# Modulation sums with buffers of their own, one visit per step of the FFN, in five pieces

## The chip, the core and the metric

The kernel runs on one core of a Trainium2 chip. The metric is the device time of one execution in microseconds. The core has five engines that run their own instruction queues side by side: PE (matrix multiply, with PEld loading its stationary operand), DVE, ACT, POOL, and SP, which here issues most DMAs. An engine works through its queue in order, so an instruction that waits holds up everything queued behind it on that engine.

## The reference, cut to what matters

Two layers of a diffusion backbone on 256 latent tokens and 256 context tokens of width 1024. Each layer is: half-step SwiGLU FFN, token mixing (attention and S5), half-step SwiGLU FFN. Every normalisation is modulated: `norm(x) * (1 + scale) + shift`, and every residual is gated. Shift, scale and gate come from the conditioning vectors:

```python
mx = (silu(c)     @ w_mod[l] + b_mod[l]).reshape(B, 9, 1, D_MODEL)   # latent tokens
mc = (silu(c_ctx) @ w_mod[l] + b_mod[l]).reshape(9, D_MODEL)         # context tokens
hx = hx + 0.5 * mx[:, 2] * swiglu(modulate(hx, norm_g[l, 0], mx[:, 0], mx[:, 1]), ffn_w_gu[l, 0], ffn_w_down[l, 0])
```

`w_mod` is 1024 x 9216 per layer in float32, 38 MB. It is multiplied with only two vectors, so it can be done as a matrix product on PE, or as a sum of rows scaled by one number per partition on other engines. The FFN is 1024 to 2 x 2816 and back to 1024 for all 512 tokens.

## The kernel before, in words

Everything is written out by hand in program order; `plan` first lists all weight loads ("units") in the order of use. A unit is one `gu` tile (gate and up columns of one of the 22 blocks of 128 hidden columns, 1 MB), one `down` tile, one piece of `w_mod`, or another weight. `take` moves on to the next unit, asks SP for later ones (`load_to`), and returns the weights. The float32 weights in `raw` are split into a high and a low part (`spl`, two buffers): ACT rounds them (L265), DVE subtracts (L266), in two halves. PE then does three products per tile (`mm3`, L312 to L314). `ahead`, called by `take`, splits the next weight unit early if it is among the next two units.

The FFN (`ffn`) runs over 22 `gu` blocks in chunks of 8, 8 and 6. A block is 48 matmuls of 128x512; then ACT makes `sl` = silu (L756), DVE multiplies to `hv` (L758), ACT rounds it (L760) and POOL subtracts (L761) to give the split `hid`. After a chunk come four `down` units. After each block and each `down`, `fillers` visits the modulation units that stand next in the plan.

Eleven of the modulation vectors (`ELEM`) are not multiplied on PE. Their units are called `dvm`. A vector has four visits of two units; each unit has two tiles of 128x512 (`draw`, 512 KB, one DMA). Per tile DVE multiplies the rows by the latent vector's numbers and adds (L530 for the first, L532), ACT multiplies by the context vector's (L535, in place), POOL adds (L537). After four units half a vector is done: the partial sums `dacc` are summed over partitions by 8 small matmuls (L547, `total`) and transposed into place (L554, `finish`), 8 and 11 steps later. There are 24 such visits in the first FFN, 4 in the second, 16 in the third. In layer 1 the vectors 5 and 7 are needed for the latent tokens alone, so ACT and POOL have nothing to do there.

A "step" (`step`) comes after every third group of products in a block. It takes one entry of `dv` (what is left of the modulation), one of `q`, or one piece of the background work `bg`, which is `s5_prep`: the S5 matrices of the layer, many small operations on DVE and long ones on POOL (E at L1027 to L1032, CL at L1055 to L1057, BL at L1076 to L1078), and matmuls on them (L1064).

`load_to(i + 3)` counts all units, `dvm` ones too, and the `draw` tiles are in three buffers in the same SP queue as the raw weights.

Of the kernel before, what the change touches and what calls it, by code (L numbers as in the profile page):

```python
# [10 lines left out]
F32 = mybir.dt.float32  # L11
F32R = mybir.dt.float32r
AF = mybir.ActivationFunctionType
OP = mybir.AluOpType
# [6 lines left out]
T = 512  # L21
# [73 lines left out]
class Net:  # L95
    def __init__(self, nc, tc, I, out, es):
        self.nc, self.tc, self.I, self.out, self.es = nc, tc, I, out, es
        pool = lambda n, b=1, **kw: es.enter_context(tc.tile_pool(name=n, bufs=b, **kw))
        sb = lambda n, b=1: es.enter_context(lines(tc, name=n, bufs=b))
        self.const = sb("const")  # L100
        self.rawp = sb("raw", 3)
        self.splp = sb("spl", 2)
        es.enter_context(tc.tile_pool(name="top", bufs=1, side="right")).tile([128, 8], F32, name="top")
        self.pacc = pool("pacc", 4, space=PSUM)
        self.pt = pool("pt", 3, space=PSUM)
        self.pm = pool("pm", 1, space=PSUM)
        self.bank, self.turn = None, 0
        self.dram = pool("dram", 1, space=DRAM)
        c = self.const
        self.k = c.tile([128, K_END], F32, name="k")  # L110
        self.ident = self.k[:, K_ID:K_ID + 128]
        self.ones = self.k[:, K_ONE:K_ONE + 128]
        self.h = c.tile([128, KT, T], F32, name="h")
        self.xn = c.tile([128, 2, KT, T], F32R, name="xn")
        self.cs = c.tile([128, KT, 38], F32, name="cs")
        self.mh = c.tile([128, 8], F32, name="mh")
        self.sel = c.tile([128, 33], F32, name="sel")
        self.mod = [c.tile([128, 9, KT, 2], F32, name=f"mod{l}") for l in range(2)]
        self.A = [c.tile([128, 3, KT, 2], F32, name=f"A{l}") for l in range(2)]
        self.smT = [c.tile([128, 128], F32, name=f"smT{l}") for l in range(2)]  # L120
        self.kg = [c.tile([128, 4], F32, name=f"kg{l}") for l in range(2)]
        self.rho8 = [c.tile([128, 16], F32, name=f"rho8{l}") for l in range(2)]
        self.units = []
        self.dv = []
        self.fp = None
        self.bg = []
        self.q = []
        self.hold = False
        self.seaming = False
# [11 lines left out]
    def plan(self):  # L141
        I = self.I
        U = self.units

        def mod_units(l, m, us=range(4)):
            for u in us:
                if (l, m) in ELEM:
                    for v in (2 * u, 2 * u + 1):
                        n0, k0 = m * 1024 + v // 4 * 512, v % 4 * 2
                        src = I["w_mod"][l].rearrange("(k p) n -> p k n", p=128)[:, k0:k0 + 2, n0:n0 + 512]  # L150
                        U.append(("dvm", (l, m, v), [(slice(0, 1024), 2, src)], False))
                    continue
                src = I["w_mod"][l].rearrange("(k p) n -> p k n", p=128)[:, :, m * 1024 + u * 256:m * 1024 + u * 256 + 256]
                U.append(("mod", (l, m, u), [(slice(0, 2048), 8, src)], False))

# [12 lines left out]

        def ffn(l, f, fill, skip=0, between=None):
            fill = list(fill)  # L170
            for c in range(3):
                for j in range(max(skip, sum(CH[:c])), sum(CH[:c + 1])):
                    gu(l, f, j)
                    if j == 0 and between:
                        mod_units(*between)
                    if fill and j:
                        mod_units(*fill.pop(0))
                for u in range(4):
                    down(l, f, c, u)
                    if fill and (c, u) < (2, 2):  # L180
                        mod_units(*fill.pop(0))
            assert not fill
# [40 lines left out]
    def load_to(self, n):  # L223
        while self.loaded < min(n, len(self.units)):
            i = self.loaded
            kind, key, srcs, sp = self.units[i]
            if kind == "dvm" and self.fp is None:
                return
            if i < 10 and kind == "mod":
                raw = self.prop.tile([128, 2048], F32, name="pmod", tag="pmod", bufs=5)  # L230
            elif kind == "dvm":
                raw = self.fp.tile([128, 1024], F32, name="draw", tag="draw", bufs=3)
            else:
                raw = self.rawp.tile([128, 2048], F32, name="raw", tag="raw")
            for sl, k, src in srcs:
                if sl is None:
                    dst = raw.rearrange("p (k g n) -> p k g n", k=8, g=2)[:, :, k, :]
                elif sl == "glu":
                    dst = raw[16 * k:16 * k + 16, 0:1024].rearrange("p (b n) -> p b n", b=2)
                else:  # L240
                    dst = raw[:, sl].rearrange("p (k n) -> p k n", k=k)
                self.nc.sync.dma_start(dst, src)
            self.raws[i] = raw
            self.loaded += 1
# [24 lines left out]
    def take(self, kind, key, ahead=True):  # L269
        i = self.cur  # L270
        assert self.units[i][0] == kind and self.units[i][1] == key, (self.units[i][:2], kind, key)
        self.cur += 1
        if self.hold:
            self.load_to(min(i + 8, 11))
        else:
            self.load_to(i + 3)
        self.split(i)
        if ahead and not self.hold:
            self.ahead()
        self.raws.pop(i - 1, None)  # L280
        self.spl.pop(i - 1, None)
        return self.spl[i] if self.units[i][3] else self.raws[i]
# [43 lines left out]
    def step(self, n=1):  # L326

        for _ in range(n):
            if self.dv:
                g = self.dv.pop(0)  # L330
                if g:
                    g()
            f = self.q.pop(0) if self.q else None
            if f is not None:
                f()
            else:
                self.tick()
# [6 lines left out]

    def dv_flush(self):
        while self.dv:
            g = self.dv.pop(0)
            if g:
                g()

    def drain(self):
        while self.bg:
# [159 lines left out]
            us = [u] if alone else range(4)  # L512
            self.q.append(lambda: self.mod_finish(l, m, us, e))

    def dvm_unit(self, l, m, v):

        nc = self.nc
        half, r = v // 4, v % 4  # L520
        raw = self.take("dvm", (l, m, v)).rearrange("p (k n) -> p k n", k=2)
        ss = (1,) if l and m > 4 else (0, 1)
        if r == 0:
            self.dacc = {s: self.fp.tile([128, 512], F32, name=f"dacc{s}", tag=f"dacc{s}", bufs=2) for s in ss}
        acc = self.dacc
        for i in range(2):
            c0, c1 = (self.cs[:, 2 * r + i, 6 + s:7 + s] for s in range(2))
            first = r == i == 0
            if first:
                nc.vector.tensor_scalar(acc[1], raw[:, i], c1, None, op0=OP.mult)  # L530
            else:
                nc.vector.scalar_tensor_tensor(acc[1], raw[:, i], c1, acc[1], op0=OP.mult, op1=OP.add)  # L532
            if 0 in ss:
                x = acc[0] if first else raw[:, i]
                nc.scalar.activation(x, raw[:, i], AF.Copy, scale=c0)  # L535
                if not first:
                    nc.gpsimd.tensor_tensor(acc[0], acc[0], x, op=OP.add)  # L537
        if r < 3:
            return
        st = {}  # L540

        def total():
# [16 lines left out]
            nc.vector.tensor_tensor(dst.rearrange("p (j a) s -> p a j s", a=2), t, bc(b, [128, 2, 2, 2]), op=OP.add)  # L559
            self.mod_derived(l, m, k0, k0 + 4)  # L560

        self.dv_flush()
        self.dv += [None] * 7 + [total, None, None, finish]

    def mod_derived(self, l, m, k0, k1):
        nc = self.nc
# [166 lines left out]
    def ffn(self, l, f, halves, started, nxt=None):  # L733
# [3 lines left out]
        gate = 2 if f == 0 else 8  # L737
        hid = {}
        with lines(self.tc, name=f"ffn{l}{f}", bufs=1) as fp:
            self.fp = fp  # L740
            j0 = 0
            for ci, nf in enumerate(CH):
                for j in range(j0, j0 + nf):
# [10 lines left out]
                                    self.step()  # L754
                    sl = fp.tile([128, T], F32, name="sl", tag="sl", bufs=1)
                    nc.scalar.activation(sl[:, c], pg[:, c], AF.Silu)  # L756
                    hv = fp.tile([128, T], F32, name="hv", tag="hv", bufs=2)
                    nc.vector.tensor_tensor(hv[:, c], sl[:, c], pu[:, c], op=OP.mult)  # L758
                    hd = fp.tile([128, 2, T], F32R, name="hid", tag="hid", bufs=8)
                    nc.scalar.activation(hd[:, 0, c], hv[:, c], AF.Copy)  # L760
# [7 lines left out]
                    self.sq_begin()  # L768
                early = None
                if lastc:  # L770
                    self.dv_flush()
                for u in range(4):
                    w = early or self.take("down", (l, f, ci, u))
                    w = w[:, :, 0:nf * 256].rearrange("p s (k n) -> p s k n", k=nf)
# [22 lines left out]
                            self.step()  # L797
                    if ci == 0 and u == 0:
                        self.flush()
                    for i in range(2):  # L800
                        n = 2 * u + i
                        for s in halves:
# [31 lines left out]
    def s5_prep(self, l):  # L834
# [6 lines left out]
        with lines(self.tc, name=f"prep{l}", bufs=1, side="right") as pp:  # L841
# [4 lines left out]
            dma(par[0:16], I["s5_lam_re"][l].rearrange("d (a b) p -> (d a) (b p)", b=2))  # L846
            dma(par[32:48], I["s5_lam_im"][l].rearrange("d (a b) p -> (d a) (b p)", b=2))
            dma(ldt[64:80], I["s5_log_dt"][l].rearrange("d (a b) -> (d a) b", b=2))
            bl = [pp.tile([128, 16, 16], F32, name=f"bl{i}") for i in range(2)]
            for i, nm in enumerate(("s5_b_re", "s5_b_im")):  # L850
                nc.sync.dma_start(bl[i], I[nm][l].rearrange("d (a b) p m -> (b p) (d a) m", b=2))
            cr = pp.tile([128, 4, 2, 2, 64], F32, name="cr", tag="W")
# [824 lines left out]
```

## Time and profile before

| | us |
|---|---|
| median of 3 runs | 2185.57 (2183.81 to 2187.68) |
| the profiled execution | 2195.32 |
| its span, first to last instruction | 2193.5 |
| PE busy | 1984.7 (90%) |
| DVE busy | 1109.0 (51%) |
| ACT busy | 784.7 (36%) |
| POOL busy | 767.9 (35%) |

The mean granted clock of PE is 0.938 of full speed. Busy shares are averages over stages with different limits: the FFNs of the first layer run from about 50 to 545 us and from about 880 to 1270 us, those of the second from about 1290 to 1740 and from 2000 us on, and token mixing lies between.

### The profile page before, as it was taken

The page shows a single profiled execution, that of the slowest core. Times are in us where ns is not written, and L with a number is a line of the kernel's source. Part 1 is how long each engine was busy: PE and PEld are TensorE (multiplying, and loading weights), DVE is VectorE, ACT ScalarE, POOL GpSimd, SP SyncE. Part 2 cuts the span into 40 slices and gives each one's busy share as a digit, 9 for nine tenths or more (in the row PEclk, how much of TensorE's full clock was granted, in tenths as well). Part 3 has the DMA queues.
Part 4 walks back from the last instruction along what each step waited for, and adds up shares of the span by engine and source line. Part 5 has one row for each costly group of instructions (what it writes and reads, how often), then busy time and mean ns, then how long its engine had stood idle before and what let it go on. Part 6 is the DMA issues. An engine that isn't in the chain of part 4 may idle for free. (4 is left out here: it accounts for less than half of the span.)

```text
span 2193.5 us, 27710 instructions
## 1 busy us (share of the span) xinstructions
PE 1984.7 (90%) x10839; PEld 1600.1 (73%) x10839; DVE 1109.0 (51%) x1777; ACT 784.7 (36%) x1283; POOL 767.9 (35%) x789
## 2 busy tenths in 40 slices
PE   7788778889999999989999997778899999899999
PEld 5656556667889568768888875555678888668999
DVE  6566433543655774343332455555543465575554
ACT  4432333332435553331222343321222343455443
POOL 2348766431444404140100224864520244503000
PEclk9888888899999999989999998888899999899999
DMA  7533444454443103443333354344463344308663
GB/s 257 139 116 130 140 135 146 131 162 134 121 157 101 39 4 112 124 143 98 96 96 87 106 140 116 115 134 144 148 188 87 101 132 144 88 20 235 188 190 118
DMA packets 342278, 277.73 MB, mean 127 GB/s; under 512 B 30558, under 2 KB 311460, under 8 KB 342148
## 3 DMA queue, kind: packets, MB, share of 16 engines
q1 hardware_dynamic: 339184, 268.44, 41.2%
q0 software_dynamic: 1888, 7.31, 0.9%
q8 instruction: 85, 1.39, 0.3%
q14 instruction: 45, 0.37, 0.1%
q10 hardware_dynamic: 1076, 0.22, 0.1%
HBM read 263.39 MB, written 12.55 MB: 126 GB/s over the span
## 5 line engine op out<-in xcount | busy, mean ns | idle before, releaser
L312 PE MATMUL acc<-xn,spl 128*128 128x512 f32 (+1 forms) x1664 | 625.3, 376 | 96.3 <-ACT spl L265 87.9
L314 PE MATMUL acc<-xn,spl 128*128 128x512 f32 (+1 forms) x1664 | 617.2, 371 | 20.7 <-DVE spl L266 20.7
L313 PE MATMUL acc<-xn,spl 128*128 128x512 f32 (+1 forms) x1664 | 611.6, 368 | 1.9 <-DVE xn L429 0.2
L266 DVE TENSOR_TENSOR spl<-raw,spl 128x1024 fp32r<-128x1024 f32 (+2 forms) x312 | 391.9, 1292 | 231.5 <-ACT spl L265 229.6
L312 PEld LDWEIGHTS acc<-xn,spl 128*128 128x128 f32 x1664 | 329.0, 198 | 164.9 <-ACT spl L265 98.7
L265 ACT ACTIVATE spl<-raw 128x1024 fp32r<-128x1024 f32 (+3 forms) x344 | 323.8, 989 | 260.3 <-PE acc L314 138.5
L314 PEld LDWEIGHTS acc<-xn,spl 128*128 128x128 f32 x1664 | 327.4, 197 | 89.0 <-DVE spl L266 40.0
L761 POOL TENSOR_TENSOR hid<-hv,hid 128x512 fp32r<-128x512 f32 (+1 forms) x88 | 102.1, 1160 | 783.9 <-ACT hid L760 783.8
L313 PEld LDWEIGHTS acc<-xn,spl 128*128 128x128 f32 x1664 | 329.1, 198 | 54.6 <-DVE xn L658 4.3
L312 PE MATMUL acc<-hid,spl 128*128 128x512 f32 (+1 forms) x740 | 273.3, 369 | 28.8 <-ACT spl L265 28.8
L314 PE MATMUL acc<-hid,spl 128*128 128x512 f32 (+1 forms) x740 | 270.0, 365 | 10.5 <-DVE spl L266 10.5
L313 PE MATMUL acc<-hid,spl 128*128 128x512 f32 (+1 forms) x740 | 268.8, 363 | 0.0
L758 DVE TENSOR_TENSOR hv<-sl,acc 128x512 f32<-128x512 f32 (+1 forms) x88 | 54.6, 621 | 391.5 <-PE acc L314 344.6
L537 POOL TENSOR_TENSOR dacc<-dacc,draw 128x512 f32<-128x512 f32 x126 | 187.2, 1485 | 158.7 <-ACT draw L535 106.8
L822 DVE SCALAR_TENSOR_TENSOR h<-acc,mod,h 128x256 f32<-128x256 f32 x192 | 84.8, 478 | 226.4 <-PE acc L314 226.4
L760 ACT ACTIVATE hid<-hv 128x512 fp32r<-128x512 f32 (+1 forms) x88 | 50.8, 577 | 391.1 <-DVE hv L758 391.1
L312 PEld LDWEIGHTS acc<-hid,spl 128*128 128x128 f32 x740 | 144.0, 195 | 55.4 <-ACT spl L265 32.5
L314 PEld LDWEIGHTS acc<-hid,spl 128*128 128x128 f32 x740 | 144.3, 195 | 37.4 <-DVE spl L266 16.5
L532 DVE SCALAR_TENSOR_TENSOR dacc<-draw,cs,dacc 128x512 f32<-128x512 f32 x154 | 164.0, 1065 | 4.7
L313 PEld LDWEIGHTS acc<-hid,spl 128*128 128x128 f32 x740 | 144.5, 195 | 20.0
L266 POOL TENSOR_TENSOR spl<-raw,spl 128x768 fp32r<-128x768 f32 (+3 forms) x32 | 65.5, 2047 | 213.7 <-ACT spl L265 204.0
L535 ACT ACTIVATE draw<-draw,cs 128x512 f32<-128x512 f32 x126 | 91.0, 724 | 131.4 <-DVE dacc L532 83.2
(390 smaller groups left out, 2355.5 us busy)
## 6 DMA issues: line engine op xcount, KB each, us to landing
raw<-in_ffn_w_gu SPq DMA_DIRECT2D x176, 512.0 KB
draw<-in_w_mod SPq DMA_DIRECT2D x88, 512.0 KB
raw<-in_ffn_w_down SPq DMA_DIRECT2D x32, 1024.0 KB
raw<-in_w_mod SPq DMA_DIRECT2D x20, 1024.0 KB
raw<-in_ffn_w_down SPq DMA_DIRECT2D x16, 768.0 KB
raw<-in_w_in SPq DMA_DIRECT2D x16, 768.0 KB
pmod<-in_w_mod SPq DMA_DIRECT2D x8, 1024.0 KB
raw<-in_w_out SPq DMA_DIRECT2D x8, 1024.0 KB
```

Of the source, the lines that this page charges most:

```text
L265: nc.scalar.activation(s[:, 0, a:b], raw[:, a:b], AF.Copy)
L266: (nc.gpsimd if mix and b == n else nc.vector).tensor_tensor(s[:, 1, a:b], raw[:, a:b], s[:, 0, a:b].bitcast(F32), op=OP.subtract)
L312: mm(out, sl[0], sr[0], start=start, stop=False)
L313: mm(out, sl[0], sr[1], start=False, stop=False)
L314: mm(out, sl[1], sr[0], start=False, stop=stop)
L532: nc.vector.scalar_tensor_tensor(acc[1], raw[:, i], c1, acc[1], op0=OP.mult, op1=OP.add)
L535: nc.scalar.activation(x, raw[:, i], AF.Copy, scale=c0)
L537: nc.gpsimd.tensor_tensor(acc[0], acc[0], x, op=OP.add)
L758: nc.vector.tensor_tensor(hv[:, c], sl[:, c], pu[:, c], op=OP.mult)
L760: nc.scalar.activation(hd[:, 0, c], hv[:, c], AF.Copy)
L761: nc.gpsimd.tensor_tensor(hd[:, 1, c], hv[:, c], hd[:, 0, c].bitcast(F32), op=OP.subtract)
L822: self.nc.vector.scalar_tensor_tensor(self.h[:, n, c], ps[:, c], self.mod[l][:, gate, n, s:s + 1], self.h[:, n, c], op0=OP.mult, op1=OP.add)
```

## The change

A `dvm` unit is now one per visit, with four tiles; it no longer has loads in the list of units, and `load_to` is given a bound that counts three units other than `dvm`. The tiles of a visit are loaded by `dvm_load`, called at the start of the FFN and then at each visit for the next one, into four buffers of their own. The products and sums of a visit go into `dv` as five pieces, one per step; what is left is done at the next visit. The sum over partitions and the finish move to a list `late`, due 9 and 12 steps after the visit. To make room, `hv` has one buffer instead of two, and in `s5_prep` the two `bl` tiles share the buffers of tag "big".

```diff
@@ plan / mod_units
-                    for v in (2 * u, 2 * u + 1):
-                        n0, k0 = m * 1024 + v // 4 * 512, v % 4 * 2
-                        src = I["w_mod"][l].rearrange("(k p) n -> p k n", p=128)[:, k0:k0 + 2, n0:n0 + 512]
-                        U.append(("dvm", (l, m, v), [(slice(0, 1024), 2, src)], False))
+                    U.append(("dvm", (l, m, u), [], False))
+                    self.visits.setdefault(where[0], []).append((l, m, u))
@@ load_to / take
-            if kind == "dvm" and self.fp is None:
-                return
+            if kind == "dvm":
+                self.raws[i] = None
+                self.loaded += 1
+                continue
-                raw = self.fp.tile([128, 1024], F32, name="draw", tag="draw", bufs=3)
-            self.load_to(i + 3)
+            n, left = i, 3
+            while left and n < len(self.units):
+                left -= self.units[n][0] != "dvm"
+                n += 1
+            self.load_to(n)
@@ step
             if self.dv:
-                g = self.dv.pop(0)
-                if g:
-                    g()
+                self.dv.pop(0)()
+            for g in self.late:
+                g[0] -= 1
+            while self.late and self.late[0][0] <= 0:
+                self.late.pop(0)[1]()
@@ dvm_load, dvm_unit
+    def dvm_load(self):
+        if not self.todo:
+            return
+        l, m, u = self.todo.pop(0)
+        half, k0 = u // 2, u % 2 * 4
+        self.draws = []
+        for i in range(2):
+            raw = self.fp.tile([128, 2, 512], F32, name="draw", tag="draw", bufs=4)
+            n0 = m * 1024 + half * 512
+            self.nc.sync.dma_start(raw, self.I["w_mod"][l].rearrange("(k p) n -> p k n", p=128)[:, k0 + 2 * i:k0 + 2 * i + 2, n0:n0 + 512])
+            self.draws += [raw[:, 0], raw[:, 1]]
...
-        raw = self.take("dvm", (l, m, v)).rearrange("p (k n) -> p k n", k=2)
+        self.take("dvm", (l, m, u), False)
+        raws = self.draws
+        self.dv_flush()
+        self.dvm_load()
+        while r == 0 and len(self.late) > 2:
+            self.late.pop(0)[1]()
...
+        def parts(i):
+            if i < 4:
+                part1(i)
+            if i and 0 in ss:
+                part0(i - 1)
+
+        self.dv += [(lambda i=i: parts(i)) for i in range(4)]
+        if r == 0:
+            self.dv.append(lambda: parts(4))
             return
+        self.dv.append(lambda: parts(4))
...
-        self.dv_flush()
-        self.dv += [None] * 7 + [total, None, None, finish]
+        self.late.append([9, total, m])
+        self.late.append([12, finish, m])
@@ ffn
-            self.fp = fp
+            self.fp, self.todo = fp, self.visits.get((l, f), [])
+            self.dvm_load()
-                    hv = fp.tile([128, T], F32, name="hv", tag="hv", bufs=2)
+                    hv = fp.tile([128, T], F32, name="hv", tag="hv", bufs=1)
                 if lastc:
-                    self.dv_flush()
+                    self.late_flush()
                     if ci == 0 and u == 0:
                         self.flush()
+                        while any(g[2] == 2 for g in self.late):
+                            self.late.pop(0)[1]()
@@ s5_prep
-            bl = [pp.tile([128, 16, 16], F32, name=f"bl{i}") for i in range(2)]
+            bl = pp.tile([128, 2, 16, 16], F32, name="bl", tag="big", bufs=2)
+            bl = [bl[:, i] for i in range(2)]
```

## Rows read from the trace of the kernel before

**Rows 1.** The page: busy time by engine; one of the costliest groups (busy, mean ns).

```profile
PE 1984.7 (90%) x10839; PEld 1600.1 (73%) x10839; DVE 1109.0 (51%) x1777; ACT 784.7 (36%) x1283; POOL 767.9 (35%) x789
...
L537 POOL TENSOR_TENSOR dacc<-dacc,draw 128x512 f32<-128x512 f32 x126 | 187.2, 1485 | 158.7 <-ACT draw L535 106.8
```

**Rows 2.** Waits of PE, the longest: us in total, times, longest us.

```profile
PE acc L312 <- ACT spl L265: 116.7, 40, 5.5
PE acc L314 <- DVE spl L266: 31.2, 41, 1.6
PE t L1064 <- POOL CL L1057: 8.8, 2, 5.0
```

**Rows 3.** Timeline of one visit: start us, us, engine, line, operation, count, [idle before].

```profile
933.36 0.69 DVE L758 TENSOR_TENSOR hv<-sl,acc 128x512 f32<-128x512 f32 x1 [8.34 <-PE acc L314]
...
934.62 1.99 ACT L265 ACTIVATE spl<-raw 128x1024 fp32r<-128x1024 f32 x2
934.79 1.27 POOL L761 TENSOR_TENSOR hid<-hv,hid 128x512 fp32r<-128x512 f32 x1 [7.25 <-ACT hid L760]
...
935.71 0.79 PE L312 MATMUL acc<-xn,spl 128*128 128x512 f32 x1 [2.48 <-ACT spl L265]
...
937.19 0.79 PE L314 MATMUL acc<-xn,spl 128*128 128x512 f32 x1 [0.26 <-DVE spl L266]
...
938.20 4.00 DVE L532 SCALAR_TENSOR_TENSOR dacc<-draw,cs,dacc 128x512 f32<-128x512 f32 x4
938.21 0.63 PE L313 MATMUL acc<-xn,spl 128*128 128x512 f32 x1
...
938.64 0.63 PE L314 MATMUL acc<-xn,spl 128*128 128x512 f32 x1
```

**Rows 4.** Stretches: us, busy (instructions) of five engines, PE's granted clock, DMA, GB/s.

```profile
932.80:949.90 17.10, 14.35 (x49) 10.75 (x48) 7.08 (x7) 6.01 (x8) 7.31 (x5) 0.80 0.33 95
1020.00:1250.00 230.00, 230.00 (x1009) 189.20 (x1008) 76.57 (x88) 58.78 (x75) 22.07 (x17) 1.00 0.32 93
```

**Rows 5.** Three lines of the program, whole run: duration ns min/median/max.

```profile
L266 DVE TENSOR_TENSOR spl<-raw,spl x312: 681/1220/2443, 27.4 to 2181.3; 128x1024 fp32r<-128x1024 f32 x126, 128x768 fp32r<-128x768 f32 x24, 128x576 fp32r<-128x576 f32 x2, 128x864 fp32r<-128x864 f32 x2
L532 DVE SCALAR_TENSOR_TENSOR dacc<-draw,cs,dacc x154: 736/752/3533, 75.4 to 1600.6; 128x512 f32<-128x512 f32 x154
L537 POOL TENSOR_TENSOR dacc<-dacc,draw x126: 1262/1300/2167, 77.0 to 1457.5; 128x512 f32<-128x512 f32 x126
```

**Rows 6.** Waits of SP's DMA queue, the second longest.

```profile
SPq L242 <- POOL dacc L537: 545.6, 61, 28.5
```

**Rows 7.** The five stretches with visits, columns as in rows 4 (PE, PEld, DVE, ACT, POOL).

```profile
55.00:150.00 95.00, 76.16 (x284) 57.57 (x283) 53.62 (x113) 36.90 (x52) 34.59 (x30) 0.84 0.45 125
150.00:390.00 240.00, 191.37 (x803) 142.59 (x802) 115.54 (x159) 80.33 (x111) 169.19 (x182) 0.87 0.44 136
390.00:485.00 95.00, 76.57 (x309) 57.13 (x309) 45.31 (x62) 32.06 (x44) 36.43 (x28) 0.89 0.53 159
910.00:980.00 70.00, 58.74 (x210) 43.94 (x209) 28.30 (x30) 26.19 (x36) 24.63 (x18) 0.83 0.43 128
1310.00:1600.00 290.00, 230.36 (x941) 171.62 (x939) 166.23 (x241) 76.67 (x105) 168.49 (x176) 0.86 0.44 135
```

**Rows 8.** Timeline of one sum over partitions.

```profile
154.33 0.64 PE L547 MATMUL t<-dacc,sel 128*32 128x256 f32 x8
```

**Rows 9.** The same five stretches, line L313 alone: PE and PEld.

```profile
55.00:150.00 95.00, 38.11 (x88) 19.32 (x88) 0.84 0.45 125
150.00:390.00 240.00, 92.33 (x215) 46.15 (x215) 0.87 0.44 136
390.00:485.00 95.00, 38.00 (x91) 19.04 (x90) 0.89 0.53 159
910.00:980.00 70.00, 29.60 (x67) 14.98 (x66) 0.83 0.43 128
1310.00:1600.00 290.00, 111.78 (x258) 55.48 (x257) 0.86 0.44 135
```

More of the change, by code (lines that the diff above doesn't have):

```diff
@@ L123, in __init__ @@
         self.units = []
-        self.dv = []
+        self.dv, self.late = [], []
         self.fp = None
@@ L143, in plan @@
         U = self.units
+        self.visits, where = {}, [None]
         def mod_units(l, m, us=range(4)):
@@ L170, in ffn @@
             fill = list(fill)
+            where[0] = (l, f)
             for c in range(3):
@@ L226, in load_to @@
             kind, key, srcs, sp = self.units[i]
-            if kind == "dvm" and self.fp is None:
-                return
+            if kind == "dvm":
+                self.raws[i] = None
+                self.loaded += 1
+                continue
             if i < 10 and kind == "mod":
                 raw = self.prop.tile([128, 2048], F32, name="pmod", tag="pmod", bufs=5)
-            elif kind == "dvm":
-                raw = self.fp.tile([128, 1024], F32, name="draw", tag="draw", bufs=3)
             else:
@@ L346, in dv_flush, with late_flush @@
         while self.dv:
-            g = self.dv.pop(0)
-            if g:
-                g()
+            self.dv.pop(0)()
+    def late_flush(self):
+        self.dv_flush()
+        while self.late:
+            self.late.pop(0)[1]()
     def drain(self):
@@ L513, in mod_unit, with dvm_unit @@
             self.q.append(lambda: self.mod_finish(l, m, us, e))
-    def dvm_unit(self, l, m, v):
+    def dvm_load(self):
[9 more added lines that the diff above has]
+            self.draws += [raw[:, 0], raw[:, 1]]
+    def dvm_unit(self, l, m, u):
         nc = self.nc
-        half, r = v // 4, v % 4
-        raw = self.take("dvm", (l, m, v)).rearrange("p (k n) -> p k n", k=2)
+        half, r = u // 2, u % 2
+        self.take("dvm", (l, m, u), False)
+        raws = self.draws
         ss = (1,) if l and m > 4 else (0, 1)
+        self.dv_flush()
+        self.dvm_load()
+        while r == 0 and len(self.late) > 2:
+            self.late.pop(0)[1]()
         if r == 0:
@@ L525, in dvm_unit, with part1, part0 @@
         acc = self.dacc
[L526 to L530, printed above, removed]
-            else:
[L532 to L538, printed above, removed]
+        def part1(i):
+            c1 = self.cs[:, 4 * r + i, 7:8]
+            if r == i == 0:
+                nc.vector.tensor_scalar(acc[1], raws[i], c1, None, op0=OP.mult)
+            else:
+                nc.vector.scalar_tensor_tensor(acc[1], raws[i], c1, acc[1], op0=OP.mult, op1=OP.add)
+        def part0(i):
+            c0 = self.cs[:, 4 * r + i, 6:7]
+            x = raws[i] if r or i else acc[0]
+            nc.scalar.activation(x, raws[i], AF.Copy, scale=c0)
+            if r or i:
+                nc.gpsimd.tensor_tensor(acc[0], acc[0], x, op=OP.add)
+        def parts(i):
[6 more added lines that the diff above has]
+            self.dv.append(lambda: parts(4))
             return
+        self.dv.append(lambda: parts(4))
         st = {}
@@ L799, in ffn @@
                         self.flush()
+                        while any(g[2] == 2 for g in self.late):
+                            self.late.pop(0)[1]()
                     for i in range(2):
```

## The prediction

> **What bounds the kernel now.** I read the page first, then who waited for whom on PE, then the timeline of one stall, then tables by stretch. The page shows PE busy for 1984.7 of 2193.5 us [rows 1], so a change to the side work can only pay through PE's own stalls and its clock. PE's waits have one owner: 116.7 us until ACT has written the first half of a split weight (L265) and 31.2 us until DVE has written its remainder (L266), some 40 times each [rows 2]; nothing else is above 10 us. The timeline shows one such stall [rows 3]: when a unit's last matmul is done, DVE makes hv (933.36), then ACT splits the next weights (from 934.62), PE starts at 935.71, waits again for DVE's remainder until 937.19, and then takes 0.43 us per matmul (938.21 to 938.64). From 1020 to 1250 us, where no scaled sums run, PE takes 230 us for 1009 instructions, 0.228 each, at a granted clock of 1.00; the unit with the stall has 0.80 [rows 4]. So a stall costs its gap and then a spell at the lower of the two clock levels (1.2 instead of 2.4 GHz).
>
> A unit of 48 matmuls with a visit of the scaled sums behind it takes 17.10 us [rows 4]; without, 48 x 0.228 = 10.94. The difference, 6.16 us, is there once per visit, and the plan has 44 of them: 24 in the first FFN, 4 in the second, 16 in the third.
>
> Why it is there can be read in the code. `ahead` splits a unit only if it is among the next two. Before, a visit is two units (v = 2u, 2u+1), so the next weights are third in line and their split is left to the visit itself, behind hv and hid. In the clean stretch the next weights are at most second.
>
> **The change part by part.**
> One unit per visit, and a visit that doesn't split (`take(..., False)`): the next weights are now second in line, and their split is issued when the current unit is taken, a unit's time (11 us) before PE wants it. This is the edit that pays: up to 44 x 6.16 = 271 us if nothing else becomes late.
>
> Load window: three weight units ahead instead of three units of any kind, so the raw weights are asked for earlier. The split can't move without it. It costs no instruction.
>
> Scaled sums in five pieces: the same DVE, ACT and POOL instructions (four sums, four scalings, three or four adds per visit), handed out one piece per step. PE waits for none of them before the sum over partitions, so the order costs nothing while DVE and POOL have a unit's time for a visit's work: DVE 2 x 1.22 + 4 x 0.75 + 0.69 = 6.1 us, POOL 3.5 x 1.30 + 1.27 = 5.8 us, each alone [rows 3, 5]. What it costs where that cover is gone is the next part.
>
> Draws loaded at the visit before, two of 512 KB into four buffers: as many DMAs and bytes as now. On SP they stand in front of the next raw loads and wait for the last add and sum of the visit before. SP already waits 545.6 us for these adds [rows 6]. The ends: a gain (a draw no longer holds up a raw load within the visit), or a loss of POOL's backlog at each visit. I take zero, because the raw weights are asked for two units ahead; the loss is rival C. Traffic becomes 2.1 MB per 10.94 us, 192 GB/s, against at most 159 in a visited stretch now [rows 7]: a late DMA is kept in the upper end.
>
> The sum over partitions comes 9 steps after a visit and its finish 12 (before, 8 and 11): the same 8 small matmuls, 0.64 us [rows 8]. But the last piece is now issued only 4 steps before its sum, so PE would stand there for POOL: nothing if POOL is less than some 9 us behind, the rest of its backlog otherwise; I take nothing here and count POOL's load below. One hv buffer instead of two: DVE waits for POOL's remainder of the unit before, 1.27 us of work [rows 3] that starts a unit earlier; nothing unless POOL is a whole unit behind. b in the "big" buffers: read long before its buffer is wanted, nothing.
>
> **What is late next.** PE's floor in the five stretches with visits is three times the count of L313 [rows 9] at 0.228 us, and PE's other instructions of [rows 7] at 0.08 (0.64 for eight): 62, 160, 65, 47 and 190 us, 524 in place of 790. But POOL is busy 169.2 us in the second stretch and 168.5 in the fifth, DVE 115.5 and 166.2 [rows 7]: the preparation of S5 runs there too, paced by PE's steps, and is compressed with them. And DVE and POOL slow each other: four sums, 0.752 each at the median [rows 5], take 4.00 us with POOL's adds beside them [rows 3], and an add has a median of 1.300 and a mean of 1.485 [rows 1, 5].
>
> If DVE's splits and sums could not overlap with POOL at all, a visit would cost DVE 2 x 1.22 + 4 x 0.752 = 5.45 us on top of POOL's time. The second stretch holds 13 visits and 3.5 x 13 adds, which would be 0.185 shorter each: 169.2 - 8 + 71 = 232 us. The fifth holds 16; its preparation is lengthened too, and I take 150 us for POOL (an estimate, 11% off): 150 + 87 = 237. The other three, with little but visits, would be some us over their floor: 75, 70 and 50. What the rows show lies between full overlap and none, so I take the middle of floor and sum: 68, 196, 68, 49 and 214 = 595 us, 195 saved.
>
> The profiled execution took 2195.32 us, its span of 2193.5 and 1.8 around it; 2195.3 - 195 = 2000. It stood 0.45% above the median of the runs, 2185.57, so the median to expect is 2000 x 0.9956 = 1992 us.
>
> **The rivals.**
> A, PE's floor is reached everywhere. For it: PE waited for POOL (L1064) only 8.8 us in all [rows 2], and DVE and POOL have idle time in every stretch [rows 7]. Against: in the second, POOL's 169 us already exceed the floor of 160. 2195.3 - 266 = 1929, so 1921 us.
>
> B, DVE and POOL exclude each other, and the sums above hold: 75 + 232 + 70 + 50 + 237 = 664, 126 saved, 2069, so 2060 us. For it: the lengthened sums and adds. Against: in the fifth stretch the two are busy 334.7 us within 290 [rows 7], and it still moves on.
> [...]
>
> C, slower: SP becomes the bound. A draw load waits for POOL, the raw loads behind it wait too, and PE stands once POOL is further behind than the raw weights' lead, about a unit and a half or 16 us. It decides where POOL needs more than the present time per visit, 530/29 = 18.3 us in the second and fifth stretch. POOL has 169.2/13 = 13.0 us of work per visit; were all of it lengthened like its longest add against the mean (2.167 to 1.485), 18.9. Then 29 visits lose 0.6 us each, the other 15 gain nothing: 2213, so 2203 us. Against: POOL's 13.0 us hold much of that lengthening already.
>
> D, the split is issued early but runs late, since ACT stands before it for raw weights or in a piece: the stall stays, 2186 us. Against: in the clean stretch, with the same order, PE shows no gap [rows 4].
>
> **How the numbers follow.** Forecast 0.50 (its own range 1957 to 2026, half the way to A and to B), A 0.17, B 0.26, C 0.04, D 0.03. The likeliest gives 1992 us. The range takes in most of A and of B: 1930 to 2060. 0.2%, some 4 us, is what a measurement of this kernel tells from no change: faster 0.93, same 0.03, slower 0.04.
>
> **What would show it.** PE's waits for L265 and L266 fall from 148 us to under 40, and the granted clock of the visited stretches rises from 0.83 to 0.89 to above 0.95. L265 runs while PE is still in the unit before. L532's and L537's means rise. Where PE still waits, it is at L1064 or L547 for POOL, in the middle of the first and third FFN, and POOL is busy over 85% there. The forecast is wrong if the stretch from 910 to 980 us, which has no preparation, doesn't come down to about 49 us, or if L265 comes to wait for DMA at most visits.

## The result, and the profile after

The changed kernel takes 2035.68 us (median of 4 runs, 2031.85 to 2037.62) against 2186.62 of the kernel before in the same comparison (4 runs, 2183.81 to 2189.53). The ratio is 0.9307 (95% interval 0.9287 to 0.9328), so 151 us are saved. The time lies in the range, 44 us above the predicted 1992, beyond the forecast's own range (to 2026) and below rival B's 2060.

The page after: busy time by engine, and two of the costliest groups (busy, mean ns, then idle before them).

```profile
PE 1900.4 (94%) x10839; PEld 1556.5 (77%) x10839; DVE 1141.5 (56%) x1777; ACT 780.2 (38%) x1283; POOL 798.4 (39%) x789
...
L566 POOL TENSOR_TENSOR dacc<-dacc,draw 128x512 f32<-128x512 f32 x126 | 188.4, 1496 | 94.4 <-ACT draw L564 59.0
L559 DVE SCALAR_TENSOR_TENSOR dacc<-draw,cs,dacc 128x512 f32<-128x512 f32 x154 | 183.0, 1188 | 3.5
```

The instruction counts are those of [rows 1]; what changed is when the instructions run. L557, L559, L564 and L566 are the old L530, L532, L535 and L537; L316 to L318 the old L312 to L314; L586 the old L547; L1107 and L1100 the old L1064 and L1057.

PE's waits after (us in total, times, longest):

```profile
PE t L1107 <- POOL CL L1100: 57.2, 8, 17.8
PE b L586 <- POOL dacc L566: 6.1, 1, 6.1
...
PE acc L317 <- POOL hid L801: 4.2, 1, 4.2
PE t L593 <- ACT mev L588: 3.9, 2, 3.3
PE t L586 <- POOL dacc L566: 3.7, 1, 3.7
...
PE acc L318 <- DVE spl L266: 2.2, 5, 0.8
```

The two waits that owned the list in [rows 2], 148 us for L265 and L266, are gone: 2.2 us for DVE's remainder, and L265 is not in the list down to 1.5 us. In their place stands one that was 8.8 us before, PE's matmul of the S5 preparation waiting for POOL's CL, now 57.2.

One visit in the second FFN after (start us, us, engine, line, operation, count, [idle before]), to be laid beside [rows 3]:

```profile
845.46 1.99 ACT L265 ACTIVATE spl<-raw 128x1024 fp32r<-128x1024 f32 x2
846.54 2.61 DVE L266 TENSOR_TENSOR spl<-raw,spl 128x1024 fp32r<-128x1024 f32 x2 [1.65 <-ACT spl L265]
849.58 3.43 DVE L559 SCALAR_TENSOR_TENSOR dacc<-draw,cs,dacc 128x512 f32<-128x512 f32 x3
851.17 4.38 POOL L566 TENSOR_TENSOR dacc<-dacc,draw 128x512 f32<-128x512 f32 x3 [4.23 <-ACT draw L564]
852.50 3.44 SPq L534 DMA_DIRECT2D draw<-in_w_mod  x2
855.19 0.69 DVE L798 TENSOR_TENSOR hv<-sl,acc 128x512 f32<-128x512 f32 x1 [2.17 <-PE acc L318]
856.45 1.99 ACT L265 ACTIVATE spl<-raw 128x1024 fp32r<-128x1024 f32 x2
```

The split for the next unit runs at 845.46, 9.7 us ahead of this unit's hv (855.19). In [rows 3] it came 1.3 us behind hv, with PE already standing. Sums and adds lie under the matmuls.

The visited stretches after, bounded so that each holds the work of its counterpart in [rows 7]: each edge is the matmul of L317 that has the same number in PE's order as the matmul of L313 at the edge before. Columns as in [rows 4] (PE, PEld, DVE, ACT, POOL busy, granted clock, DMA, GB/s):

```profile
54.90:123.30 68.40, 64.36 (x282) 50.97 (x281) 42.87 (x95) 30.96 (x43) 24.48 (x21) 0.98 0.68 191
123.30:346.60 223.30, 176.54 (x804) 135.90 (x803) 150.20 (x178) 83.85 (x119) 194.06 (x188) 0.89 0.50 152
346.60:411.80 65.20, 65.20 (x307) 52.05 (x306) 48.09 (x59) 31.14 (x43) 43.66 (x30) 1.00 0.68 206
837.90:885.00 47.10, 47.10 (x213) 38.04 (x213) 25.88 (x28) 22.27 (x31) 20.37 (x15) 1.00 0.53 161
1213.90:1442.50 228.60, 197.49 (x938) 154.92 (x937) 166.81 (x242) 74.53 (x105) 172.17 (x173) 0.93 0.55 166
```

PE has the instruction counts of [rows 7] here, within three, so the prediction's floor holds as it stands: 62, 160, 65, 47 and 190 us. The third and fourth stretches are at their floor, at a granted clock of 1.00, and the first is 6 us over it. The second is 63 us over: PE stands 47 us (223.30 less 176.54) and works 17 us longer than the floor. The fifth is 39 over: 31 standing, 8 longer.

Where the second stretch stands, in the timeline (POOL's rows between two of PE's; same columns as above):

```profile
191.80 0.39 PE L318 MATMUL acc<-hid,spl 128*128 128x512 f32 x1
193.08 2.25 POOL L566 TENSOR_TENSOR dacc<-dacc,draw 128x512 f32<-128x512 f32 x1
195.29 1.59 POOL L1070 TENSOR_TENSOR te<-E,Pn 128x256 f32<-128x256 f32 x1
...
208.56 1.40 POOL L1100 TENSOR_TENSOR CL<-te,te 128x576 f32<-128x576 f32 x1 [0.96 <-DMA ed<-E]
210.01 0.64 PE L1107 MATMUL t<-CL,BB 128*32 128x128 f32 x2 [17.82 <-POOL CL L1100]
```

PE stands 17.8 us while POOL works through adds (L566) and the pieces of E (L1070 to L1075) before it comes to the CL that PE's next instruction wants. The stretches before and behind the pause (columns as above) show what it costs beside itself:

```profile
170.00:191.80 21.80, 21.14 (x100) 16.59 (x98) 17.20 (x26) 7.83 (x11) 20.63 (x33) 1.00 0.48 136
210.00:215.00 5.00, 0.69 (x6) 0.23 (x9) 0.00 (x0) 0.00 (x0) 4.82 (x4) 0.50 0.53 162
215.00:220.00 5.00, 5.00 (x24) 3.73 (x25) 0.88 (x2) 1.01 (x2) 4.63 (x5) 0.50 1.07 329
```

The granted clock is 1.00 (2.4 GHz) before the pause and 0.50 (1.2 GHz) in the two stretches behind it.

### The profile page after: what moved, and what is told of

Same layout as the page of the kernel before. It is cut to its first block, busy times and chain, and to the rows that moved or that the text cites. A ratio compares the mean times of both kernels' runs of the same rounds, so it can differ in the third digit from the quotient of the medians.

```text
span 2032.3 us, 27700 instructions
## 1 busy us (share of the span) xinstructions
PE 1900.4 (94%) x10839; PEld 1556.5 (77%) x10839; DVE 1141.5 (56%) x1777; ACT 780.2 (38%) x1283; POOL 798.4 (39%) x789
## 5 line engine op out<-in xcount | busy, mean ns | idle before, releaser
L316 PE MATMUL acc<-xn,spl 128*128 128x512 f32 (+1 forms) x1664 | 600.8, 361 | 8.6 <-ACT mv L1478 5.9
L317 PE MATMUL acc<-xn,spl 128*128 128x512 f32 (+1 forms) x1664 | 592.9, 356 | 1.9 <-DVE xn L438 0.2
L318 PE MATMUL acc<-xn,spl 128*128 128x512 f32 (+1 forms) x1664 | 592.0, 356 | 1.9 <-DVE spl L266 1.9
L266 DVE TENSOR_TENSOR spl<-raw,spl 128x1024 fp32r<-128x1024 f32 (+2 forms) x312 | 409.1, 1347 | 207.9 <-ACT spl L265 206.0
L265 ACT ACTIVATE spl<-raw 128x1024 fp32r<-128x1024 f32 (+3 forms) x344 | 323.7, 989 | 217.6 <-PE acc L318 184.9
L801 POOL TENSOR_TENSOR hid<-hv,hid 128x512 fp32r<-128x512 f32 (+1 forms) x88 | 107.8, 1225 | 662.8 <-ACT hid L800 662.7
L316 PEld LDWEIGHTS acc<-xn,spl 128*128 128x128 f32 x1664 | 315.7, 190 | 66.8 <-issue 10.8
L317 PEld LDWEIGHTS acc<-xn,spl 128*128 128x128 f32 x1664 | 315.7, 190 | 50.6 <-DVE xn L697 4.3
L318 PEld LDWEIGHTS acc<-xn,spl 128*128 128x128 f32 x1664 | 315.8, 190 | 50.0 <-DVE spl L266 4.1
L317 PE MATMUL acc<-hid,spl 128*128 128x512 f32 (+1 forms) x740 | 265.0, 358 | 4.2 <-POOL hid L801 4.2
L316 PE MATMUL acc<-hid,spl 128*128 128x512 f32 (+1 forms) x740 | 267.7, 362 | 0.0
L318 PE MATMUL acc<-hid,spl 128*128 128x512 f32 (+1 forms) x740 | 264.7, 358 | 0.3 <-DVE spl L266 0.3
L566 POOL TENSOR_TENSOR dacc<-dacc,draw 128x512 f32<-128x512 f32 x126 | 188.4, 1496 | 94.4 <-ACT draw L564 59.0
L559 DVE SCALAR_TENSOR_TENSOR dacc<-draw,cs,dacc 128x512 f32<-128x512 f32 x154 | 183.0, 1188 | 3.5
L564 ACT ACTIVATE draw<-draw,cs 128x512 f32<-128x512 f32 x126 | 91.0, 723 | 196.7 <-DVE dacc L559 152.3
L317 PEld LDWEIGHTS acc<-hid,spl 128*128 128x128 f32 x740 | 141.6, 191 | 24.4 <-POOL hid L801 5.3
L316 PEld LDWEIGHTS acc<-hid,spl 128*128 128x128 f32 x740 | 141.8, 192 | 23.5 <-issue 4.2
L318 PEld LDWEIGHTS acc<-hid,spl 128*128 128x128 f32 x740 | 141.6, 191 | 20.8 <-DVE spl L266 0.7
L266 POOL TENSOR_TENSOR spl<-raw,spl 128x768 fp32r<-128x768 f32 (+3 forms) x32 | 66.1, 2064 | 209.6 <-ACT spl L265 209.6
```

Source lines behind the costliest of these rows:

```text
L265: nc.scalar.activation(s[:, 0, a:b], raw[:, a:b], AF.Copy)
L266: (nc.gpsimd if mix and b == n else nc.vector).tensor_tensor(s[:, 1, a:b], raw[:, a:b], s[:, 0, a:b].bitcast(F32), op=OP.subtract)
L316: mm(out, sl[0], sr[0], start=start, stop=False)
L317: mm(out, sl[0], sr[1], start=False, stop=False)
L318: mm(out, sl[1], sr[0], start=False, stop=stop)
L559: nc.vector.scalar_tensor_tensor(acc[1], raws[i], c1, acc[1], op0=OP.mult, op1=OP.add)
```

## The experiments

The theory after the result: the early split removed the stall, and what is left of the 271 us possible is POOL, overloaded where the preparation of S5 runs. The rivals asked which part of the change was needed, and whether POOL's own load or its contention with DVE was the rest. All ratios are against the kernel before, run beside each experiment.

**The early split alone.** On the kernel before, the load window and the look-ahead of `ahead` are each one unit longer where visits stand between:

```diff
-            self.load_to(i + 3)
+            self.load_to(i + 3 + any(u[0] == "dvm" for u in self.units[i:i + 3]))
...
-        n = min(j + 2, len(self.units))
+        n = min(j + 2 + (j < len(self.units) and self.units[j][0] == "dvm"), self.loaded)
```

> The kernel before, with one thing of the change alone: the next weights may be third in line when they are asked for and split, behind the two half visits. The draws stay in three buffers in SP's queue, the sums stay in a burst at the visit, the sum over partitions 8 steps later. Theory (the early split is what pays): PE's waits for L265 and L266 fall from 148 us to under 40 us and the time to 2020 to 2080 us. Rival (the draws' own buffers and the pieces carry half of the gain or more): the raw weights come late behind the draws, waits for L265 stay above 75 us, time 2100 to 2190 us.

It takes 2214.26 us, ratio 1.0105 (1.0083 to 1.0126): 1% slower than before, beyond the range of either expectation. Waits of PE, and of ACT for raw weights:

```profile
PE acc L312 <- ACT spl L265: 112.1, 22, 11.5
...
ACT spl L265 <- DMA raw<-in_ffn_w_gu: 242.2, 33, 17.3
ACT spl L265 <- DMA raw<-in_ffn_w_down: 130.9, 14, 16.8
```

PE still waits 112.1 us for ACT's split, in 22 pauses of up to 11.5 us where [rows 2] has 40 of up to 5.5, because ACT now waits 373 us for the raw weights (90 before, 7.5 after the whole change). The timeline of one visit shows why:

```profile
967.51 2.00 ACT L265 ACTIVATE spl<-raw 128x1024 fp32r<-128x1024 f32 x2 [6.29 <-DMA raw<-in_ffn_w_gu]
972.25 0.72 ACT L535 ACTIVATE draw<-draw,cs 128x512 f32<-128x512 f32 x1
973.53 6.53 POOL L537 TENSOR_TENSOR dacc<-dacc,draw 128x512 f32<-128x512 f32 x4
977.01 0.37 SPq L242 DMA_DIRECT2D draw<-in_w_mod  x1
977.79 0.99 SPq L242 DMA_DIRECT2D raw<-in_ffn_w_gu  x2
984.76 2.00 ACT L265 ACTIVATE spl<-raw 128x1024 fp32r<-128x1024 f32 x2 [6.48 <-DMA raw<-in_ffn_w_gu]
```

Read it backwards: the split at 984.76 waits for the raw load issued at 977.79; that stood on SP behind a draw load (977.01), which waits for a free draw buffer, so for this visit's adds (from 973.53); these wait for ACT's scaling (972.25), which stood on ACT behind the split before (967.51), itself waiting for raw weights. With three draw buffers and two draws per visit the loop closes within this visit.

**A fourth draw buffer, with and without the split.** The first run has the edit above and this one together, the second this one alone:

```diff
-                raw = self.fp.tile([128, 1024], F32, name="draw", tag="draw", bufs=3)
+                raw = self.fp.tile([128, 1024], F32, name="draw", tag="draw", bufs=4)
...
-                    hv = fp.tile([128, T], F32, name="hv", tag="hv", bufs=2)
+                    hv = fp.tile([128, T], F32, name="hv", tag="hv", bufs=1)
...
-            bl = [pp.tile([128, 16, 16], F32, name=f"bl{i}") for i in range(2)]
+            bl = pp.tile([128, 2, 16, 16], F32, name="bl", tag="big", bufs=2)
+            bl = [bl[:, i] for i in range(2)]
```

> e1 (the kernel before with the early split) plus room: a fourth draw buffer, paid for as in the change with one hv buffer and the shared bl. Loads stay in the plan's order, the sums in a burst. Theory (with three buffers the second draw waits for this visit's own adds, which stand on ACT behind the very split whose raw weights are queued behind that draw; a fourth buffer makes it wait for the visit before): ACT's waits for raw weights fall from 373 us to under 60, PE's waits for L265 from 112 us to under 30, time 2030 to 2075 us. Rival (the raw weights are asked for too late in this order, whatever the buffers): PE's waits for L265 above 70 us, time above 2120 us.

> The kernel before with the fourth draw buffer alone (and what pays for it: one hv buffer, the shared bl); the split stays where it was, at the visit behind hid. Theory (the two edits need each other): the waits for late raw weights (90 us on ACT) go, so the longer of PE's gaps shrink to the plain 2.5 us, but every visit keeps its stall and its spell of the lower clock: waits for L265 and L266 still 110 to 150 us, time 2140 to 2190 us. Rival (late raw weights were the better part of the loss, and the buffer alone heals it): below 2110 us.

Together they take 2037.76 us, ratio 0.9308 (0.9281 to 0.9335): the whole gain of the change. The buffer alone takes 2172.32, ratio 0.9918 (0.9894 to 0.9941). Waits with both, then with the buffer alone:

```profile
PE t L1065 <- POOL CL L1058: 39.4, 6, 12.0
...
PE acc L312 <- ACT spl L265: 6.5, 4, 2.8
...
ACT spl L265 <- DMA raw<-in_ffn_w_gu: 42.8, 15, 9.5
```

```profile
PE acc L312 <- ACT spl L265: 88.4, 32, 7.3
PE acc L314 <- DVE spl L266: 40.6, 42, 2.6
...
ACT spl L265 <- DMA raw<-in_ffn_w_gu: 7.6, 5, 3.5
```

The table of two by two, against some 2189 us before: split alone +24, buffer alone -18, both -150. The buffer alone takes ACT's waits for raw weights away but leaves the stall; the split alone moves the stall to the raw weights. The gain belongs to the pair.

**Three parts of the change undone**, one at a time: the pieces issued all at once at the visit; the draws loaded at their own visit; the load window back at three units of any kind, visits counted too. With one unit per visit that still takes in the next weights, so only the third weight unit goes.

```diff
-        self.dv += [(lambda i=i: parts(i)) for i in range(4)]
+        for i in range(5):
+            parts(i)
```

> The changed kernel, but the five pieces of a visit are issued at once at the visit instead of one per step. Theory (the order of the pieces costs and gives next to nothing, POOL's load sets the loss): within 10 us of the changed kernel, 2025 to 2046 us. Rival (the pieces keep hv, hid and the preparation from standing behind a burst): slower by 20 to 60 us, 2055 to 2095 us, with PE waiting again for L265 or L266.

```diff
-        raws = self.draws
...
         self.dvm_load()
+        raws = self.draws
...
-            self.dvm_load()
```

> The changed kernel, but the four tiles of a visit are loaded at that visit, not one visit ahead (four buffers as before, the pieces wait for the DMA). Theory (the buffers matter for SP, the lead of the draws hardly does, as their landing of some 7 us fits into a unit of 11): 2030 to 2060 us. Rival (the sums start late, ACT's scalings stand in front of silu and hid until the draws land): PE waits for ACT or for dacc above 40 us more, time 2075 to 2130 us.

```diff
-            n, left = i, 3
+            n, left = i, 3 - any(u[0] == "dvm" for u in self.units[i:i + 3])
```

> The changed kernel, but where scaled sums run the raw weights are asked for two weight units ahead instead of three (as far as the split needs, no more). Theory (the raw weights' lead is what lets the early split run on time): ACT waits for raw weights again, PE's waits for L265 rise from under 2 us to above 40, time 2070 to 2150 us. Rival (the draws in buffers of their own are enough): within 12 us of the changed kernel.

The burst takes 2044.09, ratio 0.9328 (0.9309 to 0.9346): 8 us more than the change, with the intervals touching, and PE waits 13.0 us for L265 and 6.6 for L266 again. So the pieces are worth little. The same-visit loads take 2031.75, ratio 0.928 (0.9252 to 0.9308), and the short window 2033.86, ratio 0.9282 (0.9258 to 0.9306): neither the visit ahead nor the third weight unit is worth anything that can be measured. With the short window ACT waits 34.1 us for raw weights instead of 7.5:

```profile
ACT spl L265 <- DMA raw<-in_ffn_w_gu: 22.3, 9, 4.3
ACT spl L265 <- DMA raw<-in_ffn_w_down: 11.8, 4, 6.2
```

PE doesn't see it. So my theory that the third unit's lead carries the split was wrong; a window that doesn't reach the next weights wasn't run.

**What is left: POOL's adds or DVE's sums.** Each kernel leaves out work that the result needs, so its time only says what that work costs.

```diff
-            if r or i:
-                nc.gpsimd.tensor_tensor(acc[0], acc[0], x, op=OP.add)
```

> The changed kernel without POOL's adds of the context vector's sums (only the first of eight scaled tiles enters them). POOL loses 188 us of work. Theory (PE's remaining loss is POOL's work in the stretches with the preparation of S5): waits of PE for the CL tiles fall from 57 us to under 15, those for dacc and hid are gone, the clock's spells with them; time 1935 to 1960 us. Rival 1 (the few steps between CL and the matmuls on it are too short whatever else POOL does): the waits stay above 30 us, time above 1985 us. Rival 2 (DVE and POOL exclude each other): it gains too, but then e4 gains as well.

```diff
-            else:
-                nc.vector.scalar_tensor_tensor(acc[1], raws[i], c1, acc[1], op0=OP.mult, op1=OP.add)
```

> The changed kernel without DVE's scaled sums of the latent vector beyond the first tile (L559 is left out, 183 us of DVE), POOL's adds stay. Rival 2 (DVE and POOL exclude each other): POOL's add falls from a mean of 1.50 us to 1.35 or less, PE's waits for CL by more than half, time 1960 to 2000 us. Theory (POOL's own load is enough): POOL is shortened by some 30 us over the run, the waits fall by less than 25 of 57 us, time 2005 to 2030 us.

Without the adds: 1966.43 us, ratio 0.8975 (0.8961 to 0.899), 69 us better than the change and 6 above what the theory allowed. Without the sums: 1988.57, ratio 0.9076 (0.9058 to 0.9094), 47 better, in the rival's range. The wait for CL and the row of the sums without the adds; then, without the sums, the row of the adds in the page and the wait for CL:

```profile
PE t L1105 <- POOL CL L1098: 29.3, 5, 11.5
...
L559 DVE SCALAR_TENSOR_TENSOR dacc<-draw,cs,dacc 128x512 f32<-128x512 f32 x154 | 159.0, 1033 | 3.5
```

```profile
L564 POOL TENSOR_TENSOR dacc<-dacc,draw 128x512 f32<-128x512 f32 x126 | 173.7, 1379 | 54.2 <-ACT draw L562 28.0
```

```profile
PE t L1105 <- POOL CL L1098: 36.0, 6, 12.4
```

CL's wait (57.2) falls to 29.3 and 36.0, and in neither case goes: the theory expected under 15 without the adds, the rival a fall by more than half without the sums, where an add was to come to 1350 ns at most and has 1379. With the sums out, POOL, whose instructions are unchanged, is busy 35 us less (763.4 against 798.4), so contention is real; but whether POOL's load is the smaller or the larger part isn't separated by these two, since each takes both a load and its contention away. Neither theory holds alone.

**More time for CL.** Three more steps between CL's store and the matmuls on it:

```diff
+                    yield
+                    yield
+                    yield
```

> The changed kernel with three more steps between POOL's CL tiles and the matmuls on them (12 more steps of the preparation per layer, all still within the FFN). Theory (POOL lacks throughput there; 12 steps of some 2.3 us give it that much more time per layer): PE's waits for CL fall from 57 us to 15 to 35, time 1990 to 2015 us. Rival (only the distance in steps is short, POOL has the time): waits below 10 us, time 1950 to 1980 us. Other rival (POOL's backlog shows wherever PE next touches it): waits for dacc, hid and BL take over, time within 10 us of the changed kernel.

It takes 2021.98, ratio 0.923 (0.9206 to 0.9253), 14 us better. PE's longest waits:

```profile
PE t L586 <- POOL dacc L566: 24.1, 4, 14.3
PE b L586 <- POOL dacc L566: 22.0, 2, 15.6
```

CL is off the list, and PE stands for POOL at the sum over partitions instead, 46.1 us (9.8 in the change). The place of the wait can be moved; POOL's backlog shows at the next point where PE touches it. That was the other rival's account, though its time, within 10 us of the change, was missed by 4. The theory's 15 to 35 us at CL and 1990 to 2015 us didn't come.

**Less work for POOL and DVE.** A vector that is not in `ELEM` is multiplied on PE, by eight small matmuls per MB of `w_mod` (16 instructions in the trace). All of them on PE, in the changed kernel and in the kernel before; and 24 of the 44 visits on PE:

```diff
-ELEM = ((0, 2), (0, 4), (0, 3), (0, 5), (0, 7), (0, 6), (1, 0), (1, 4), (1, 3), (1, 5), (1, 7))
+ELEM = ()
```

> The changed kernel with an empty list of vectors for the scaled sums: all 44 visits are matmuls on PE, as the remaining modulation units are, 16 small ones in 1.07 us each. PE's work grows by 44 x 1.07 = 47 us over the floor of 1921, POOL and DVE are free of the sums. Theory (the sums cost PE more through POOL and DVE than the matmuls would): 1965 to 1990 us, waits for CL under 15 us. Rival (the 44 units now share the three raw buffers and SP waits for PE to free them, so raw weights come late): waits for L265 or for the raw modulation weights above 30 us, time above 2010 us.

> The kernel before with an empty list of vectors for the scaled sums, nothing of the change. Theory (the stall comes from visits of two units and from the sums; without them `ahead` and the window serve as they are): as the changed kernel with all on PE, 1958 to 1972 us. Rival (the pieces of the change that remain without sums, the window and one hv buffer, matter): above 1980 us.

```diff
+ELEM = ((0, 7), (0, 6), (1, 0), (1, 5), (1, 7))
```

> The changed kernel with 24 visits on PE (those that fall in the stretches with the preparation of S5) and 20 as scaled sums (vectors 7 and 6 of layer 0, 0, 5 and 7 of layer 1). Theory: the sums cost nothing where POOL has no preparation, so only 24 x 1.07 = 26 us stand over the floor of 1921: 1945 to 1970 us, 10 to 25 us below the kernel with all on PE. Rival (sums cost about as much as the matmuls everywhere): within 8 us of the kernel with all on PE.

All on PE: 1964.24, ratio 0.8968 (0.8949 to 0.8987); the kernel before with the same line: 1965.01, ratio 0.8979 (0.8945 to 0.9013), so without visits nothing of the change matters. Some on PE is the fastest of all: 1955.09, ratio 0.8926 (0.8908 to 0.8944), 81 us under the change and 9 under all on PE, where the theory had 10 to 25 and the rival at most 8. Its page, its wait for CL, and the stretch from 55 to 420 us (columns as above):

```profile
PE 1893.6 (97%) x11115; PEld 1548.5 (79%) x11115; DVE 1014.3 (52%) x1678; ACT 712.9 (37%) x1181; POOL 652.9 (33%) x705
```

```profile
PE t L1107 <- POOL CL L1100: 3.6, 3, 2.0
```

```profile
55.00:420.00 365.00, 361.46 (x1864) 281.10 (x1863) 179.06 (x291) 120.09 (x163) 177.63 (x191) 1.00 0.60 180
```

PE has 276 instructions more than in the changed kernel and is busy 6.8 us less, since it runs at a granted clock of 1.00 through a stretch where the first three rows of the change show 0.98, 0.89 and 1.00.

## Why the prediction was right, and where it was not

**The stall, its size and the clock behind it: right.** 148 us of waits became some 2. The stretch in the second FFN, foreseen at 49 us, took 47: of 4 x 6.16 = 24.6 us for its four visits, which have no preparation beside them, 23.5 came back. The clock passed 0.95 in three stretches (0.98, 1.00, 1.00), not in the two with the preparation (0.89, 0.93).

**What is late next: right in place.** PE's remaining waits are those named, L1064 (57.2 us, all in the second and fifth stretch) and L547 (9.8). POOL is busy 87% of the second stretch, as foreseen, but 75% of the fifth, where I said over 85. L532's mean rises, from 1065 to 1188 ns; L537's hardly does (1485 to 1496).

**The term of the sum that was mis-sized: the middle between floor and sum.** The five stretches now take 68, 223, 65, 47 and 229 us, 633 together, where I had 68, 196, 68, 49 and 214, 595. The second is 27 us and the fifth 15 us over; the others are met or beaten by up to 3. Of the 161 us between the profiled executions (spans 2193.5 and 2032.3) the stretches hold 158.

The two are nearer to rival B's 232 and 237 than to mine. Is it B's mechanism? Busy time can't say, since an instruction that is held up counts as busy. The lengths can. In the trace after, the sums (L559) that no POOL instruction overlaps take 752 ns at the median, those that POOL covers almost wholly 1666; an add (L566) takes 1289 ns alone and 1636 covered by DVE. At the length that each kind of instruction has alone (medians over this trace and those of five experiments on the changed kernel, an estimate), POOL's work in the second stretch comes to 160 us and DVE's sums and remainders to 72: 232 if they excluded each other. The stretch took 223, with POOL idle for 29 of them. So they don't exclude each other, but most of their overlap is lost: their instructions overlap for 135 us there, and last 93 us longer in all than alone. How much of my 42 us in these two stretches is this, and how much the next point, no run separates. The Trainium skill's GPSIMD Engine Reference, 1. Specifications, puts POOL's SBUF interfaces in contention with DVE's instructions of two SBUF inputs, as the sums are. The trace agrees, with 1666 against 752.

What I left out of the sum is that PE's order is fixed. A backlog on POOL stops PE at the next matmul that needs it, however much idle time POOL has later, and the pause brings the lower clock. In the second stretch that is 36.4 us in five waits for CL. The floor's terms held; averaging over a stretch didn't.

**The step that was wrong: buffers of the draws at zero, the load window as the split's condition.** I wrote that the early split "is the edit that pays" and "can't move without" the window, and took zero for the buffers. The runs show otherwise for both: the third weight unit of the window is worth nothing, and the split without the fourth buffer costs 24 us instead of paying 150. The point was in [rows 6]: SP already waited 545.6 us for POOL's adds. I asked what stood behind that wait, but only for the buffers of after, not what the fourth one removed. Rival D, a split that is issued early and runs late, is what the early split alone does, though the whole change escapes it. That the time came out in spite of this step is luck: the change held the buffer to which the sum gave no worth.

The costs taken as nothing for the pieces and for loading one visit ahead were right within some 8 us.

**Open:** how the rest divides between POOL's load, contention and PE's order, and what the shorter `hv` and shared `bl` cost beside visits (they were in both runs with four draw buffers; with all on PE, the kernel with them and the one without take the same time).

## What to carry to other kernels

Before an instruction is moved earlier, follow its inputs back through every in-order queue: where a DMA waits for a buffer whose release stands behind the instruction that is to be moved, the move can turn the wait into a loop, and one more buffer is then part of the edit. Work taken off the busiest engine is free only while its helpers keep up at each point where PE touches them: judge a helper there, not by its busy share of the run (POOL 39%). Here a better split of the work (1955 us) beat a better order of it (2036), and with the work back on PE the order no longer mattered.

## What was not expected of the hardware

The two side engines slow each other in both directions, and by much: with POOL beside it from start to end a sum takes 1666 ns instead of 752. Without POOL's adds a sum on DVE has a mean of 1033 ns, with them 1188; without DVE's sums an add has 1379, with them 1496. And PE's own busy time falls with its pauses: it took 1984.7 us for 10839 instructions before, 1900.4 after, and 1880.7 without POOL's adds, at a mean granted clock of 0.938, 0.966 and 0.979, for the same number of instructions.
